# One K tile to a ring tile, 64 bytes behind its head: the split weights of MLA's non-rotary queries and keys

## The chip, the core and the metric

The kernel runs on one core of a Trainium2 chip (8 cores). The core has TensorE (PE; its weight loads are shown as PEld), VectorE (DVE), ScalarE (ACT), GpSimd (POOL) and SyncE (SP), whose queue issues most transfers here. The metric is the device time of one execution in microseconds: 1142.42 us, the median of three runs (1142.38 to 1142.46).

## The reference, cut to what matters

One encoder layer on 256 tokens of width 2048: parallel MLA and differential attention, then cross-attention into 256 memory tokens, a SwiGLU and a final norm, all in float32. The change touches the two up-projections of MLA without rotation:

```
q  = (rms_norm(c_q)  @ w_uq ).reshape(b, s, 8, 128 + 64)    # c_q: 512 wide
q_nope, q_rope = q[..., :128], apply_rope(q[..., 128:], cos_r, sin_r)
kv = (rms_norm(c_kv) @ w_ukv).reshape(b, s, 8, 128 + 128)   # c_kv: 256 wide
k_nope, v_mla = kv[..., :128], kv[..., 128:]
s  = q_nope . k_nope + q_rope . k_rope ;  p = softmax(s * scale) ;  out = p @ v_mla
```

## The kernel before, in words

**Numbers in two halves.** Every float32 operand of a matmul is split into h (a cast to the reduced format fp32r, on ScalarE, line 107) and l (the rest, a subtraction on VectorE, line 108). A product is then three matmuls, in lines 99 to 101: h by h, and the two mixed ones. So TensorE runs three matmuls for each tile of a product, and every weight passes through ScalarE and VectorE before it.

**Weights.** `weights()` (line 124) loads a piece from HBM into a staging buffer `wraw` of 2048 columns, three of which exist, through SP's queue in program order. It then splits it into ring tiles `wh` and `wl` of 1024 columns, four of each. `step` says how many K tiles (128 rows of the contraction) share a ring tile: with 512 columns to a K tile, two. A ring tile is free again when the last matmul that reads it is over; a staging buffer, when the last split that reads it is.

**MLA's up-projections** (lines 605 to 626). First `w_uq_r` (rotary queries, four K tiles, ring tiles wh_791 and wh_795 in the program's numbers) through `project()`, into the PSUM tiles acc_787 and acc_788; the rope of the queries (lines 494 to 498, on VectorE) turns these into qr. Then for each half hg of the heads: `w_uq_n` (four K tiles of 512 columns), `w_ukv_k` (two) and `w_ukv_v` (two). The first two go through `stationary()`: there the weights are the operand that is loaded into TensorE and the transposed activations (cqT, 256 columns) stream past. For each of four heads and each K tile it runs three matmuls of 256 columns: 48 matmuls for qT and 24 for kT per half, 144 in all for both halves. Two heads share one PSUM tile, which is split into qT or kT when all of its matmuls are over. `w_ukv_v` goes through `project()`, where weights stream (512 columns, 12 matmuls).

**Scores.** For each head `scores()` (psc), `softmax()` (maximum on VectorE, exponentials of line 641 on ScalarE, the scaling of e in line 663 on VectorE), `prob_T()` (the transposes ppt, line 652) and `heads_out()` (po). The differential attention's projections (acc from x0T, "dk" the first of those behind) are independent of them.

**What sets the order.** A scheduler goes over the recorded program and orders each engine's instructions by its own estimate of when their operands will be there. Every engine then takes its instructions strictly in that order. Transfers keep the program's order on SP's queue.

Of the kernel before, what the change touches and what calls it, by code (L numbers as in the profile page):

```python
# [12 lines left out]
F32R = mybir.dt.float32r  # L13
# [6 lines left out]
P = 128  # L20
# [60 lines left out]
def encoder_block(ctx: ExitStack, tc: tile.TileContext, a, out):  # L81
# [3 lines left out]
    wp = ctx.enter_context(tc.tile_pool(name="wp", bufs=3))  # L85
# [11 lines left out]
    def mm(o, l, r, start, stop):  # L97

        nc.tensor.matmul(o, l.h, r.h, start=start, stop=False)  # L99
        nc.tensor.matmul(o, l.h, r.l, start=False, stop=False)  # L100
        nc.tensor.matmul(o, l.l, r.h, start=False, stop=stop)  # L101
# [3 lines left out]
    def split_into(dst, src, scale=None, by_vector=False):  # L105
        if scale is None:
            last_cast[0] = nc.scalar.copy(out=dst.h, in_=src).ins  # L107
            last_split[0] = nc.vector.tensor_tensor(out=dst.l, in0=src, in1=dst.h.bitcast(F32), op=ALU.subtract).ins  # L108
        else:
            if by_vector:  # L110
                nc.vector.tensor_scalar(out=dst.h, in0=src, scalar1=scale, scalar2=None, op0=ALU.mult)
            else:
                nc.scalar.activation(dst.h, src, AF.Copy, scale=scale)
            nc.vector.scalar_tensor_tensor(
                out=dst.l, in0=src, scalar=scale, in1=dst.h.bitcast(F32), op0=ALU.mult, op1=ALU.subtract
            )

    def act_tile(shape=(P, 4, S), name="act"):
        return Split(
            act.tile(list(shape), F32R, name=name + "_h", tag="act"),  # L120
            act.tile(list(shape), F32R, name=name + "_l", tag="act"),
        )

    def weights(src, fine=False, pool=None, before_k=None, cut=None, raw=None):

        nk, ncols = src.shape[1:]
        begun = raw is not None  # L130
        if not begun:
            raw = wp.tile([P, 2048], F32, name="wraw", tag="wraw", bufs=3)
        raw = raw[:, :nk * ncols].rearrange("p (k c) -> p k c", k=nk)
        step = 1 if fine else nk
        for k in range(0, nk, step):
            if before_k is not None:
                before_k(k)
            if begun and k == 0:
                continue
            tc.keep_in_program_order(nc.sync.dma_start(out=raw[:, k:k + step, :], in_=src[:, k:k + step, :]))  # L140
        ks = []
        step = max(1, 1024 // ncols // 2 * 2)
        for k in range(0, nk, step):
            n = min(step, nk - k)
            if pool:
                w = pool((P, n, ncols), "w")
            else:
                w = [wp.tile([P, 1024], F32R, name=x, tag=x, bufs=4)[:, :n * ncols].rearrange("p (k c) -> p k c", k=n)
                     for x in ("wh", "wl")]
                w = Split(*w)  # L150
            if fine:
                for j in range(n):
                    for c in ([slice(0, ncols)] if cut is None else [slice(0, cut), slice(cut, ncols)]):
                        split_into(w[:, j, c], raw[:, k + j, c])
            else:
                split_into(w, raw[:, k:k + n, :])
            ks += [w[:, j, :] for j in range(n)]
        return ks

    def project(actT, pieces, before=None, fine=0):  # L160

        accs = [acc_tile() for _ in range(NT)]
        ncols = pieces[0].shape[2]
        nk = sum(src.shape[1] for src in pieces)
        kt = 0
        for i, src in enumerate(pieces):
            if before is not None:
                before(i)
            for w in weights(src, i < fine):
                x = actT(kt)  # L170
                for tt in range(NT):
                    mm(accs[tt][:, :ncols], x[tt] if isinstance(x, tuple) else x[:, tt * P:(tt + 1) * P], w,
                       start=kt == 0, stop=kt == nk - 1)
                kt += 1
        return accs
# [4 lines left out]
    def nat(name):  # L180
        pool, bufs = nat_pool
        return pool.tile([P, 512], F32, name=name, tag="nat", bufs=bufs)
# [8 lines left out]
    def ps_tile(name):  # L191
        pool, tag = banks[1]
        return pool.tile([P, 512], F32, name=name, tag=tag)
# [239 lines left out]
    for i in range(8):  # L433
        one_by_one = i < 3
        if not one_by_one:
            x0T.load(i // 2, i % 2 * 2, 2)
        if i == 3:
            tc.keep_in_program_order(nc.sync.dma_start(out=posi, in_=a["pos"]))
            tc.keep_in_program_order(nc.sync.dma_start(out=invf, in_=a["invf"].partition_broadcast(P)))
        if i >= 6:  # L440
            tc.keep_in_program_order(
                nc.sync.dma_start(out=x_res[i - 6], in_=a["x"][(i - 6) * P:(i - 5) * P, :]))
        for k, w in enumerate(weights(a["w_in_lat"][i], one_by_one,
                                      before_k=lambda k: one_by_one and x0T.load_one(2 * i + k),
                                      cut=QL if i == 0 else None, raw=lat_raw if i == 0 else None)):
            xk = x0T(2 * i + k)
            for tt in range(NT):
                x = xk[:, tt * P:(tt + 1) * P]
                mm(acc_q[tt], x, w[:, :QL], i + k == 0, i == 7 and k == 1)
                mm(acc_kv[tt][:, :LAT], x, w[:, QL:], i + k == 0, i == 7 and k == 1)  # L450
# [49 lines left out]
    def transposed(dst, src, tt, n, gain=None, raw=None):  # L500

        pt = ps_tile("pt")
        for j in range(n):
            nc.tensor.transpose(out=pt[:, j * P:(j + 1) * P], in_=src[:, j * P:(j + 1) * P], identity=ident)  # L504
        pv = pt[:, :n * P].rearrange("p (j t) -> p j t", t=P)
        if gain is not None:
            g = nat("gT").rearrange("p (j t) -> p j t", t=P) if raw is None else raw[:, :, tt * P:(tt + 1) * P]
            nc.vector.tensor_tensor(out=g[:, :n, :], in0=pv, in1=gain.unsqueeze(2).to_broadcast([P, n, P]),
                                    op=ALU.mult)
            pv = g[:, :n, :]  # L510
        split_into(dst[:, :n, tt * P:(tt + 1) * P], pv)
# [14 lines left out]
    cqT = act_tile(name="cqT")  # L526
    lat = act_tile(name="lat")
    ckvT, krT = lat[:, 0:2, :], lat[:, 2:4, :]
# [58 lines left out]
    def values(accs, r=None, n=512):  # L587

        t = act_tile((P, NT, 512), name="val")
        for tt in range(NT):  # L590
            split_into(t[:, tt, :n], accs[tt][:, :n], None if r is None else r[:, tt:tt + 1])
        return t


    def stationary(wk, xT, nk, name):

        t = act_tile(name=name)
        for hp in range(2):
            ps = ps_tile(name)
            for j in range(2):  # L600
                h = hp * 2 + j
                for kt in range(nk):
                    mm(ps[:, j * S:(j + 1) * S], wk[kt][:, h * P:(h + 1) * P], xT[:, kt, :],
                       kt == 0, kt == nk - 1)
            split_into(t[:, 2 * hp:2 * hp + 2, :], ps.rearrange("p (j t) -> p j t", j=2))
        return t
# [7 lines left out]
        qrs.append(qr)  # L614
    qT, kT, vv = [], [], []
    for hg in range(2):
        qT.append(stationary(weights(a["w_uq_n"][hg]), cqT, 4, "qT"))
        if hg == 0:
            for tt in range(NT):
                transposed(qrT, qrs[tt], tt, 4)  # L620
        kT.append(stationary(weights(a["w_ukv_k"][hg]), ckvT, 2, "kT"))
        vv.append(values(project(lambda kt: ckvT[:, kt, :], [a["w_ukv_v"][hg]])))
    mla_split = last_split[0]

# [191 lines left out]
    for tt in range(NT):  # L816
        n = nat("xk")
# [6 lines left out]
    for tt in range(NT):  # L824
        n = nat("xq")
# [113 lines left out]
    for gi, (chunks, order) in enumerate(groups):  # L939
# [5 lines left out]
        src = [a["w_dn"][h, pair0:pair0 + len(hp)] for h in range(2)]  # L945
# [145 lines left out]
```

## Time and profile before

| | |
|---|---|
| median of three runs | 1142.42 us |
| the profiled execution, its own time | 1142.48 us |
| its span | 1140.4 us |
| granted TensorE clock | 0.999 |
| TensorE busy | 1131.3 us, 5393 matmuls |
| VectorE busy | 981.0 us, 1341 instructions |
| ScalarE busy | 649.7 us, 930 instructions |
| qT: matmuls from | 71.46 us on, and again at 83.72 us |
| kT: matmuls from | 80.76 us on |

A row of the order of time has the start in us from the span's start, the length, the engine, the line, and out<-in with shapes; a bracket at the end is the engine's idle time just before and what ended it. In the grouped rows stand the count, the busy time, the mean length in ns, and the idle time before with its releasers. Lengths of matmuls include a part that overlaps the next one; the distance from start to start is what one costs.

### The profile page before, as it was taken

Reading aid. Unit: us, or ns where it says so; the run is one execution under the profiler, and the core shown is the slowest. Engines: PE = TensorE matmul, PEld = TensorE weight load, DVE = VectorE, ACT = ScalarE, POOL = GpSimd, SP = SyncE. Lnnn points to the kernel's source line nnn. Section 1 sums busy time; section 2 is a strip of 40 time slices with the busy share of each in tenths; the row PEclk is TensorE's granted clock in tenths of the full one; section 3 lists DMA queues with packets and bytes.
Section 4 is the critical chain, followed back from the end, with each engine's and each line's share of the span. In section 5 each row is a group of like instructions: output and inputs, shape, how many; then the busy total and the mean of one; then the engine's idle time right before and its main releaser. Section 6 shows DMA issues by size and latency. Waiting matters only on the chain.

```text
span 1140.4 us, 14399 instructions
## 1 busy us (share of the span) xinstructions
PE 1131.3 (99%) x5393; PEld 946.6 (83%) x5393; DVE 981.0 (86%) x1341; ACT 649.7 (57%) x930; POOL 56.4 (5%) x75
## 2 busy tenths in 40 slices
PE   9999999999999999999999999999999999999997
PEld 7888888888888888888888888888888888888886
DVE  6788766878997776989899998998999898998975
ACT  6755455556567555665555464564554664664643
POOL 4920000000001000000000000000000000000000
PEclk9999999999999999999999999999999999999999
DMA  9655334546657445455655555555555655565543
GB/s 351 243 196 183 134 117 145 182 140 227 216 202 272 153 157 182 161 211 187 216 189 216 182 196 217 185 195 211 184 203 203 209 197 195 194 242 204 192 174 129
DMA packets 35493, 222.13 MB, mean 195 GB/s; under 512 B 4320, under 2 KB 5600, under 8 KB 11104
## 3 DMA queue, kind: packets, MB, share of 16 engines
q1 hardware_dynamic: 33696, 216.60, 53.6%
q0 software_dynamic: 864, 3.15, 0.8%
q10 hardware_dynamic: 864, 1.47, 0.4%
q8 instruction: 42, 0.69, 0.2%
q14 instruction: 27, 0.22, 0.1%
HBM read 219.11 MB, written 2.10 MB: 194 GB/s over the span
## 4 chain that ended last, share of the span: by engine, by line
PE 98%; DMA 0%; issue 0%; DVE 0%; ACT 0%; SPq 0%; POOLq 0%; POOL 0%; ACTq 0%
PE acc L99 26%; PE acc L100 26%; PE acc L101 26%; PE q L99 4%; PE q L101 4%; PE q L100 4%; PE pt L504 2%; PE ppt L652 1%; PE psc L101 1%; PE psc L100 1%; PE psc L99 1%; DMA wraw<-in_w_in_lat 0%; PE acckv L99 0%; PE acckv L101 0%; PE pt L924 0%
## 5 line engine op out<-in xcount | busy, mean ns | idle before, releaser
L107 ACT CAST wh<-wraw 128x1024 fp32r<-128x1024 f32 (+2 forms) x401 | 389.4, 990 | 332.9 <-PE acc L101 290.0
L108 DVE TENSOR_TENSOR wl<-wraw,wh 128x1024 fp32r<-128x1024 f32 (+2 forms) x401 | 454.8, 1149 | 90.3 <-ACT wh L107 88.6
L107 ACT CAST wh<-tsum 128x1024 fp32r<-128x1024 f32 (+1 forms) x96 | 96.5, 1006 | 52.7 <-PE acc L101 23.0
L100 PE MATMUL acc<-wl,x2n_h 128*128 128x512 f32 x320 | 124.5, 390 | 0.0
L101 PE MATMUL acc<-wh,x2n_l 128*128 128x512 f32 x320 | 123.9, 389 | 0.0
L108 DVE TENSOR_TENSOR wl<-tsum,wh 128x1024 fp32r<-128x1024 f32 (+1 forms) x96 | 111.5, 1163 | 14.0 <-ACT wh L107 13.8
L99 PE MATMUL acc<-wh,x2n_h 128*128 128x512 f32 x320 | 109.7, 390 | 0.0
L100 PE MATMUL acc<-wl,x0T_h 128*128 128x512 f32 x224 | 88.6, 396 | 0.0
L101 PE MATMUL acc<-wh,x0T_l 128*128 128x512 f32 x224 | 88.2, 394 | 0.0
L99 PE MATMUL acc<-wh,x0T_h 128*128 128x512 f32 x224 | 86.7, 395 | 0.4 <-ACT wh L107 0.3
L100 PE MATMUL acc<-wl,hT_h 128*128 128x512 f32 x188 | 73.3, 392 | 0.0
L100 PE MATMUL q<-wl,forms_h 128*128 128x512 f32 x187 | 72.8, 389 | 0.0
L101 PE MATMUL q<-wh,forms_l 128*128 128x512 f32 x187 | 72.6, 389 | 0.0
L101 PE MATMUL acc<-wh,hT_l 128*128 128x512 f32 x188 | 72.4, 389 | 0.0
L101 PEld LDWEIGHTS acc<-wh,x2n_l 128*128 128x128 f32 x320 | 60.1, 188 | 12.4
L100 PEld LDWEIGHTS acc<-wl,x2n_h 128*128 128x128 f32 x320 | 60.1, 188 | 12.3
L99 PEld LDWEIGHTS acc<-wh,x2n_h 128*128 128x128 f32 x320 | 59.9, 188 | 12.2
L99 PE MATMUL q<-wh,forms_h 128*128 128x512 f32 x187 | 65.6, 389 | 0.0
L100 PE MATMUL acc<-wl,forms_h 128*128 128x512 f32 x167 | 64.8, 389 | 0.0
L101 PE MATMUL acc<-wh,forms_l 128*128 128x512 f32 x167 | 64.8, 389 | 0.0
L99 PE MATMUL acc<-wh,hT_h 128*128 128x512 f32 x188 | 64.5, 391 | 0.0
L99 PE MATMUL acc<-wh,forms_h 128*128 128x512 f32 x167 | 62.9, 389 | 0.0
(406 smaller groups left out, 2240.9 us busy)
## 6 DMA issues: line engine op xcount, KB each, us to landing
wraw<-in_w_gate SPq DMA_DIRECT2D x44, 1024.0 KB, 4.9
wraw<-in_w_up SPq DMA_DIRECT2D x44, 1024.0 KB, 4.8
wraw<-in_w_dn SPq DMA_DIRECT2D x41, 1024.0 KB, 4.9
wraw<-in_w_in SPq DMA_DIRECT2D x24, 1024.0 KB, 4.9
wraw<-in_w_out SPq DMA_DIRECT2D x16, 1024.0 KB, 4.9
wraw<-in_w_in_lat SPq DMA_DIRECT2D x5, 832.0 KB, 7.3
wraw<-in_w_xk SPq DMA_DIRECT2D x4, 1024.0 KB, 5.1
wraw<-in_w_xq SPq DMA_DIRECT2D x4, 1024.0 KB, 5.1
```

Source lines behind the costliest of these rows:

```text
L99: nc.tensor.matmul(o, l.h, r.h, start=start, stop=False)
L100: nc.tensor.matmul(o, l.h, r.l, start=False, stop=False)
L101: nc.tensor.matmul(o, l.l, r.h, start=False, stop=stop)
L107: last_cast[0] = nc.scalar.copy(out=dst.h, in_=src).ins
L108: last_split[0] = nc.vector.tensor_tensor(out=dst.l, in0=src, in1=dst.h.bitcast(F32), op=ALU.subtract).ins
L504: nc.tensor.transpose(out=pt[:, j * P:(j + 1) * P], in_=src[:, j * P:(j + 1) * P], identity=ident)
L652: nc.tensor.transpose(out=pt[:, kt * S + tt * P:kt * S + (tt + 1) * P], in_=p[:, tt, kt * P:(kt + 1) * P], identity=ident)
```

## The change

`weights()` gets a parameter `shift`. Where it is set, one K tile goes into each ring tile instead of two, and it begins `shift` float32 numbers behind the ring tile's head: 16 of them, 64 bytes. Both calls for `stationary()` set it, for w_uq_n and w_ukv_k in both halves. No arithmetic changes, and the staging buffers and transfers stay as they are. (An empty line that the edit adds moves every later line number by one.)

```diff
-    def weights(src, fine=False, pool=None, before_k=None, cut=None, raw=None):
+    def weights(src, fine=False, pool=None, before_k=None, cut=None, raw=None, shift=0):
...
-        step = max(1, 1024 // ncols // 2 * 2)
+        step = 1 if shift else max(1, 1024 // ncols // 2 * 2)
...
-                w = [wp.tile([P, 1024], F32R, name=x, tag=x, bufs=4)[:, :n * ncols].rearrange("p (k c) -> p k c", k=n)
-                     for x in ("wh", "wl")]
+                w = [wp.tile([P, 1024], F32R, name=x, tag=x, bufs=4)[:, shift:shift + n * ncols].rearrange(
+                    "p (k c) -> p k c", k=n) for x in ("wh", "wl")]
...
-        qT.append(stationary(weights(a["w_uq_n"][hg]), cqT, 4, "qT"))
+        qT.append(stationary(weights(a["w_uq_n"][hg], shift=16), cqT, 4, "qT"))
...
-        kT.append(stationary(weights(a["w_ukv_k"][hg]), ckvT, 2, "kT"))
+        kT.append(stationary(weights(a["w_ukv_k"][hg], shift=16), ckvT, 2, "kT"))
```

The scheduler places the instructions anew. SP's and GpSimd's orders are the same as before; those of TensorE, VectorE and ScalarE differ from this place on.

VectorE, before, ahead of the first qT matmul (wraw_837 is the staged first half of w_uq_n; kr_725 is the second token tile's rotary key, pt_734 and pt_720 transposes of keys): both subtractions of the half stand here.

```order
L108 TENSOR_TENSOR wl_840<-wraw_837,wh_839 128x1024
L498 TENSOR_TENSOR kr_725<-kr_725,ropetmp_727 128x64
L108 TENSOR_TENSOR wl_844<-wraw_837,wh_843 128x1024
L508 TENSOR_TENSOR gT_737<-pt_734,gains_101 128x256
L108 TENSOR_TENSOR lat_l_508<-pt_720,lat_h_507 128x2x128
```

So each of the two covers two K tiles, and both lie ahead of the rope of the queries.

VectorE now, in the same region but later: the half has four subtractions, and the fourth one (wl_852) stands behind the rope of the queries, whose last two steps are shown.

```order
L495 TENSOR_TENSOR ropetmp_831<-acc_788,sinr_531 128x8x32
L497 TENSOR_TENSOR qr_830<-acc_788,cosr_530 128x8x32
L108 TENSOR_TENSOR wl_852<-wraw_837,wh_851 128x512
L499 TENSOR_TENSOR qr_823<-qr_823,ropetmp_824 128x512
L499 TENSOR_TENSOR qr_830<-qr_830,ropetmp_831 128x512
L108 TENSOR_TENSOR qT_l_856<-qT_857,qT_h_855 128x512
```

The fourth subtraction moved from ahead of the keys' transposes to behind eight rope steps.

TensorE now, the 15th to the 24th matmul of qT (qT_857 and qT_884 are its two PSUM tiles; wh_847, wh_851 the third and fourth K tile): the matmul that reads wl_852 first is the 23rd.

```order
L99 MATMUL qT_884<-cqT_h_505,wh_847 128x256
L100 MATMUL qT_884<-cqT_l_506,wh_847 128x256
L101 MATMUL qT_857<-cqT_h_505,wl_848 128x256
L101 MATMUL qT_884<-cqT_h_505,wl_848 128x256
L99 MATMUL qT_857<-cqT_h_505,wh_851 128x256
L100 MATMUL qT_857<-cqT_l_506,wh_851 128x256
L99 MATMUL qT_884<-cqT_h_505,wh_851 128x256
L100 MATMUL qT_884<-cqT_l_506,wh_851 128x256
L101 MATMUL qT_857<-cqT_h_505,wl_852 128x256
L99 MATMUL qT_857<-cqT_h_505,wh_839 128x256
```

Before, the heads went one after the other there, all three matmuls of a K tile together.

TensorE before, at the first transposes of probabilities (ppt), which 57 matmuls of the dk projection (acc_1481, acc_1482) precede, the last five of them shown:

```order
L101 MATMUL acc_1482<-wh_1553,x0T_l_297 128x512
L99 MATMUL acc_1481<-wh_1553,x0T_h_296 128x512
L100 MATMUL acc_1481<-wl_1554,x0T_h_296 128x512
L101 MATMUL acc_1481<-wh_1553,x0T_l_297 128x512
L652 MATMUL ppt_1150<-ident_104,e_1142 128x128
L99 MATMUL acc_1482<-wh_1553,x0T_h_296 128x512
```

All four score tiles of the first half stood ahead of these 57.

TensorE now, at the first ppt: the second head's scores (psc_1150) stand directly ahead of it, and the dk projection (acc_1505) begins behind it.

```order
L100 MATMUL psc_1150<-lat_l_508,qrT_h_785 128x256
L101 MATMUL psc_1150<-lat_h_507,qrT_l_786 128x256
L653 MATMUL ppt_1174<-ident_104,e_1166 128x128 x4
L99 MATMUL acc_1505<-wh_1509,x0T_h_118 128x512
L100 MATMUL acc_1505<-wl_1510,x0T_h_118 128x512
```

The first head's transposes moved from behind the dk matmuls to ahead of them.

ScalarE now, the way to those transposes (kT_1079 and kT_1094 are the second half's keys; wh_1509 to wh_1543 weights of dk; e_1166 the exponentials of the first head's scores):

```order
L107 CAST wh_1509<-wraw_1507 128x1024
L107 CAST kT_h_1077<-kT_1079 128x512
L107 CAST wh_1513<-wraw_1507 128x1024
L107 CAST kT_h_1077<-kT_1094 128x512
L642 ACTIVATE e_1166,ssum_1167<-psc_1137,nm_1163 128x256 x2
L107 CAST wh_1543<-wraw_1541 128x1024
L107 CAST val_h_1129<-acc_1109 128x512
```

VectorE's scaling of e_1166 (line 664) stands behind its subtraction for wh_1543. Before, the exponentials stood behind four casts of dk weights.

## The prediction

> **What bounds the kernel now.** I read the page's busy line and its chain of waits first, then the table of stretches, then the order of time around the tiles that the change touches.
>
> ```profile
> span 1140.4 us, 14399 instructions
> PE 1131.3 (99%) x5393; PEld 946.6 (83%) x5393; DVE 981.0 (86%) x1341; ACT 649.7 (57%) x930; POOL 56.4 (5%) x75
> ...
> PE 98%; DMA 0%; issue 0%; DVE 0%; ACT 0%; SPq 0%; POOLq 0%; POOL 0%; ACTq 0%
> ```
>
> TensorE carries 98% of the chain that ended last, so the time is the number of matmuls times their pace, plus the moments in which TensorE waits. The change alters no matmul's shape or count. It can cost or win in two ways only: a wait of TensorE that appears or goes, or a different pace of the matmuls whose weights now stand elsewhere. The stretch it touches:
>
> ```profile
> 71.46:95.00 23.54, 23.54 (x177) 22.54 (x176) 21.30 (x34) 15.97 (x23) 1.56 (x2) 1.00 0.66 226
> ```
>
> In this row (stretch, its length, busy time and count of PE, PEld, DVE, ACT, POOL, then clock, DMA share, GB/s) TensorE has no gap at all: there is no wait here to be won. VectorE is busy 21.30 of 23.54 us, so there is little room for its new work. The pace, from the order of time:
>
> ```profile
> 71.46 0.28 PE L99 MATMUL qT<-cqT_h,wh 128*128 128x256 f32 x1
> ...
> 77.22 0.63 PE L99 MATMUL acc<-wh,lat_h 128*128 128x512 f32 x2
> ...
> 79.97 1.04 PE L504 MATMUL pt<-ident,qr 128*128 128x128 f32 x8
> 80.76 0.36 PE L99 MATMUL kT<-lat_h,wh 128*128 128x256 f32 x1
> ```
>
> The 48 matmuls of qT take 77.22 - 71.46 = 5.76 us, 0.120 each; the 12 of 512 columns 2.75 us, 0.229 each; the eight transposes 0.79 us.
>
> **The change, part by part.** First, the splits. Six pairs of a cast on ScalarE and a subtraction on VectorE become twelve of half the size.
>
> ```profile
> L107 ACT CAST wh<-wraw 128x1024 fp32r<-128x1024 f32 x335 | 346.0, 1052 | 273.4 <-PE acc L101 240.9 <-issue 10.8 <-PE q L101 6.4
> L107 ACT CAST wh<-wraw 128x512 fp32r<-128x512 f32 x50 | 31.0, 621 | 55.5 <-PE acc L101 49.2 <-DMA wraw<-in_w_in_lat 3.0 <-PE q L101 2.5
> L108 DVE TENSOR_TENSOR wl<-wraw,wh 128x1024 fp32r<-128x1024 f32 x335 | 404.1, 1221 | 78.8 <-ACT wh L107 77.5
> L108 DVE TENSOR_TENSOR wl<-wraw,wh 128x512 fp32r<-128x512 f32 x50 | 34.3, 686 | 7.0 <-ACT wh L107 6.6
> ```
>
> ScalarE gets 6 x (2 x 0.621 - 1.052) = 1.1 us more, VectorE 6 x (2 x 0.686 - 1.221) = 0.9 us more. Neither is on the chain by itself: TensorE's own matmuls hide them. What counts is when a split is ready.
>
> Second, the ring. Four of four pairs of ring tiles now hold one half of w_uq_n, where two did. So the fourth K tile can be cast only when the last matmul with w_uq_r (wh_795) is over, just as qT begins. Before, both splits stood long before that.
>
> ```profile
> 70.43 0.27 PE L504 MATMUL pt<-ident,kr 128*128 128x128 f32 x1
> ...
> 69.41 1.05 ACT L107 CAST wh<-wraw 128x1024 fp32r<-128x1024 f32 x1
> 70.74 0.37 ACT L107 CAST lat_h<-pt 128x256 fp32r<-128x256 f32 x1 [0.28 <-PE pt L504]
> 71.70 1.05 ACT L107 CAST wh<-wraw 128x1024 fp32r<-128x1024 f32 x1 [0.59 <-PE acc L101]
> ...
> 70.49 1.23 DVE L108 TENSOR_TENSOR wl<-wraw,wh 128x1024 fp32r<-128x1024 f32 x1 [0.74 <-ACT wh L107]
> 71.64 0.42 DVE L494 TENSOR_TENSOR ropetmp<-acc,sinr 128x256 f32<-128x256 f32 x1
> ...
> 74.62 1.22 DVE L108 TENSOR_TENSOR wl<-wraw,wh 128x1024 fp32r<-128x1024 f32 x1
> 75.75 1.29 DVE L498 TENSOR_TENSOR qr<-qr,ropetmp 128x512 f32<-128x512 f32 x2
> ...
> 327.54 1.22 DVE L108 TENSOR_TENSOR wl<-wraw,wh 128x1024 fp32r<-128x1024 f32 x1
> ...
> 328.82 0.50 PE L100 MATMUL acc<-wl,mT_h 128*128 128x512 f32 x1 [0.19 <-DVE wl L108]
> ```
>
> The casts at 69.41 and 71.70 fill ring tiles of other weights before; now they are K tiles 2 and 3 of the first half. On VectorE the rope of the queries stands between their two subtractions. The third subtraction starts at 69.41 + 0.62 + 0.03 = 70.06 and ends at 70.75. The second kr transpose comes three matmuls of 0.229 earlier, so its cast starts at 70.74 - 0.69 = 70.05, ends at 70.42, and its subtraction runs behind the third one, until about 71.1. From 71.64 to 74.62 VectorE does nine steps of this size, 0.331 each; the eight rope steps thus end at 71.1 + 2.65 = 73.75. Then the fourth subtraction: 0.69, until 74.44, and TensorE starts 0.06 later (328.82 against the end of a subtraction at 327.54 + 1.22 = 328.76, where it waited). TensorE wants it as its 23rd matmul of qT, at 71.46 + 22 x 0.120 = 74.10. **Wait one: 74.50 - 74.10 = 0.4 us.** Everything behind it on TensorE is delayed, since it takes its matmuls in order. Bounds: nothing, if VectorE runs ahead; 0.9 us, if the rope starts at 71.64 as before.
>
> The next places by the same steps: qT ends at 77.62, the transposes at 78.41, kT's first half at 79.85, the values at 82.60, kT at 84.04, the second qT at 89.80. At each place the split is ready, by 0.15 to 0.3 us at four of them: no further term, but a reason for the upper end.
>
> Third, the scores. Before, all four score tiles came late and 57 matmuls of the dk projection covered the softmax. Now the first score tile stands inside kT, and its transposes follow directly behind the second tile, before any dk matmul. ScalarE and VectorE have to be through by then.
>
> ```profile
> 76.25 0.28 PE L100 MATMUL qT<-cqT_l,wh 128*128 128x256 f32 x1
> ...
> 76.62 2.00 ACT L107 CAST wh<-wraw 128x1024 fp32r<-128x1024 f32 x2 [1.50 <-PE qT L100]
> 78.52 0.58 ACT L107 CAST qT_h<-qT 128x512 fp32r<-128x512 f32 x1
> ...
> 83.61 0.57 ACT L107 CAST kT_h<-kT 128x512 fp32r<-128x512 f32 x1
> 84.08 1.08 ACT L107 CAST val_h<-acc 128x512 fp32r<-128x512 f32 x2
> ...
> 104.61 0.46 ACT L641 ACTIVATE e<-psc,nm 128x256 f32<-128x256 f32 x1
> ...
> 105.51 0.47 ACT L641 ACTIVATE e<-psc,nm 128x256 f32<-128x256 f32 x1
> ...
> 106.07 0.62 DVE L663 TENSOR_SCALAR e<-e,rs 128x256 f32<-128x256 f32 x2
> ```
>
> In a row ScalarE needs 0.95 for a cast of 1024 (two until 78.52), 0.47 for one from PSUM (84.08 - 83.61), 0.90 for a tile's two exponentials (105.51 - 104.61). Count from T, the start of the matmul that ends the first kT tile (T is about 93.2). It ends 0.28 later, and a cast follows 0.09 after an end (76.62 against 76.25 + 0.28). Then in ScalarE's new order: kT 0.47, weights 0.95, kT 0.47, exponentials 0.90, weights 1.05; on VectorE 0.03 to start, 1.13 for the subtraction (75.75 - 74.62), 0.35 for the first half of e (0.62 for both), 0.06 to TensorE. Sum 5.78 us. TensorE reaches the transposes after 8 x 0.120 + 2.75 + 12 x 0.120 = 5.15 us. It waits 0.63, and some 0.17 more at the second transpose, whose half of e comes 0.27 later while a transpose takes 0.10. **Wait two: 0.8 us.** Bounds: 0, if ScalarE is ahead of this order; 1.2, if the transfer for its last cast is late.
>
> Fourth, the head of 64 bytes. No row of the profile has weights at such a place: in the built program every ring tile stands 64 bytes past a multiple of 128, and the shifted halves stand on one. The nearest rows are weight loads of two transposes, of x_res (96 bytes past) and e (64 past):
>
> ```profile
> L504 PEld LDWEIGHTS pt<-ident,xres 128*128 128x128 f32 x64 | 7.8, 140 | 1.8
> L652 PEld LDWEIGHTS ppt<-ident,e 128*128 128x128 f32 x64 | 7.9, 140 | 1.4
> ```
>
> Equal, so I take nothing. Bounds: 256 columns more cost 0.229 - 0.120 = 0.109, so 0.011 of a matmul of 0.120 does not scale with its columns; all of it gone from the 144 matmuls of qT and kT is 1.6 us won. On the other side the widest spread of one form is 396 against 390 ns, 144 x 0.006 = 0.9 us lost.
>
> ```profile
> L100 PE MATMUL acc<-wl,x2n_h 128*128 128x512 f32 x320 | 124.5, 390 | 0.0
> L100 PE MATMUL acc<-wl,x0T_h 128*128 128x512 f32 x224 | 88.6, 396 | 0.0
> ```
>
> [...]
>
> Sum: 0.4 + 0.8 + 0 = 1.2 us. The profiled execution took 1142.48 us, 2.1 outside the span; with 1.2 it is 1143.7, and 0.06 less against the median of 1142.42: **1143.6 us**.
>
> **Rivals.** *No wait at all*: the two waits are differences of 0.3 to 0.6 us between chains of 3 to 6 us; if the engines run that much ahead, the time stays 1142.4. For it speaks that TensorE had no gap in this stretch before; against it, VectorE's 90%.
>
> *The head quickens the loads*: 1143.6 - 1.6 = 1142.0. For it speaks the fixed 0.011 us that nothing explains; against it the two equal rows of loads. [...]
>
> *Slower: the staging buffers come free late.* The transfer of the second half of w_uq_n was issued at 67.89, when the first half's last subtraction was over; now that is 74.4. The first dk transfer was issued at 80.09; by the steps above the second half's last subtraction ends at 86.4.
>
> ```profile
> 67.89 0.33 SPq L140 DMA_DIRECT2D wraw<-in_w_uq_n  x1
> ...
> 80.09 31.71 SPq L140 DMA_DIRECT2D wraw<-in_w_in  x7
> ...
> wraw<-in_w_in SPq DMA_DIRECT2D x24, 1024.0 KB, 4.9
> wraw<-in_w_in_lat SPq DMA_DIRECT2D x5, 832.0 KB, 7.3
> ```
>
> At 4.9 us it lands at 91.3, just ahead of ScalarE's turn for it at 91.45. At 7.3, as under the load of the start, it lands at 93.7; the chain of wait two begins 1.1 us late, the next transfer adds 0.5, and the time is 1143.6 + 1.6 = 1145.2. It decides from about 6 us on. Against it: 226 GB/s here, and a median of 4.9.
>
> **Numbers.** My forecast 0.53; no wait 0.17; the quicker head 0.12; late buffers 0.18. A measurement of this kernel tells 0.2%, 2.3 us, from no change: faster means under 1140.1, slower over 1144.7. Even the quicker head without a wait (1140.8) is no change; faster is 0.03. Slower is most of the late buffers and a tail of the forecast: 0.17. The rest, 0.80, is the same. The range goes from 1141.6, the quicker head with a part of the waits, to 1145.4, late buffers.
>
> **What would show it.** Right: TensorE waits for wl (line 108) once early in qT, and for e (line 664) at the first ppt, 0.3 to 1 us each; 144 matmuls at 0.120. Wrong: no idle time of PE between 71 and 100 us (no wait), qT's 48 matmuls in under 5.4 us (the head), a cast that waits for the transfer of w_in (late buffers), or a difference that arises behind 330 us, where I assumed that nothing changes.

## The result: 0.33% slower, and the profile after

| | kernel before | changed kernel |
|---|---|---|
| median of the runs, us | 1142.28 (1141.86 to 1142.46, 6 runs) | 1145.69 (1145.09 to 1147.42, 6 runs) |
| profiled execution, us | 1142.48 | 1145.48 |
| its span, us | 1140.4 | 1143.7 |

The ratio is 1.0033, with a 95% interval from 1.0022 to 1.0043: slower, by more than the 0.2% that can be told from no change. The forecast was 1143.6 with no measurable change, in a range up to 1145.4; the median lies 0.3 us outside.

The busy line and the chain of waits of the changed kernel's page:

```profile
span 1143.7 us, 14416 instructions
PE 1132.7 (99%) x5393; PEld 947.1 (83%) x5393; DVE 981.4 (86%) x1347; ACT 648.7 (57%) x936; POOL 56.5 (5%) x75
...
PE 96%; DVE 1%; ACT 1%; issue 1%; DMA 0%; POOL 0%; POOLq 0%; SPq 0%; ACTq 0%
```

TensorE's share of the chain falls from 98 to 96%; VectorE and ScalarE enter it. The table of what TensorE waited for (70 to 103 us: total, times, longest), empty for the kernel before in this stretch, names them:

```profile
PE qT L101 <- DVE wl L108: 1.6, 2, 1.4
PE ppt L653 <- DVE e L664: 0.7, 1, 0.7
```

These idle times count from the modelled end of a matmul. What a wait costs is better read from start to start. TensorE's order of time at the three places:

```profile
73.82 0.28 PE L100 MATMUL qT<-cqT_l,wh 128*128 128x256 f32 x1
74.28 0.38 PE L101 MATMUL qT<-cqT_h,wl 128*128 128x256 f32 x1 [0.18 <-DVE wl L108]
74.50 0.28 PE L99 MATMUL qT<-cqT_h,wh 128*128 128x256 f32 x1
...
85.08 0.28 PE L101 MATMUL qT<-cqT_h,wl 128*128 128x256 f32 x1
...
86.38 0.28 PE L100 MATMUL qT<-cqT_l,wh 128*128 128x256 f32 x1
88.03 0.38 PE L101 MATMUL qT<-cqT_h,wl 128*128 128x256 f32 x1 [1.37 <-DVE wl L108]
88.25 0.28 PE L99 MATMUL qT<-cqT_h,wh 128*128 128x256 f32 x1
...
99.52 0.28 PE L101 MATMUL psc<-lat_h,qrT_l 128*128 128x256 f32 x1
100.45 0.72 PE L653 MATMUL ppt<-ident,e 128*128 128x128 f32 x4 [0.65 <-DVE e L664]
101.22 0.50 PE L99 MATMUL acc<-wh,x0T_h 128*128 128x512 f32 x1
101.56 0.40 PE L100 MATMUL acc<-wl,x0T_h 128*128 128x512 f32 x1
```

- **Pace.** From 85.08 to 86.38 eleven matmuls of qT start 0.118 us apart, where the kernel before had 0.120. Over all 144 matmuls of qT and kT the records give 2.1 ns each, 0.30 us won.
- **Wait one** (first qT): (74.50 - 73.82) - 2 x 0.118 = 0.44 us.
- **A wait in the second qT**, which the prediction did not have: (88.25 - 86.38) - 2 x 0.118 = 1.63 us.
- **Wait two** (first ppt): (100.45 - 99.52) - 0.12 = 0.81 for e. Behind it two more things follow. In the records one transpose behind another costs 0.109 and a matmul behind a transpose starts 0.028 later (7 x 0.109 + 0.028 makes the 0.79 of the eight transposes in the prediction), so four should take 0.36 to the next matmul's start. They take 0.77: 0.12 more between the first three, the second of which waits for its half of e, and 0.29 more behind the last. The 0.29 is a wait of its own, which the table above leaves out because it stands at a weight load: the first dk matmul has to wait until VectorE has read its accumulator for val_l. That matmul then takes 0.34 instead of 0.23, 0.11 more. Together 0.81 + 0.12 + 0.29 + 0.11 = 1.33 us.

```profile
101.22 0.19 PEld L99 LDWEIGHTS acc<-wh,x0T_h 128*128 128x128 f32 x1 [0.29 <-DVE val_l L108]
```

At all three places the first matmul behind the wait costs 0.10 to 0.11 us more than its pace (0.22 instead of 0.118 twice, 0.34 instead of 0.23); this is counted above.

So 0.44 + 1.63 + 1.33 - 0.30 = 3.10 of the 3.3 us by which the span grew; the remaining 0.2 is a sum of small gaps of both signs elsewhere, the largest at 284 us (0.57 more than the pace, where TensorE waits for a cast) and at 328 us (0.35 less).

What held the second qT stands in VectorE's order of time, and behind it GpSimd's and SyncE's queue (a view each, in this order):

```profile
73.54 0.69 DVE L108 TENSOR_TENSOR wl<-wraw,wh 128x512 fp32r<-128x512 f32 x1
...
77.34 2.60 DVE L108 TENSOR_TENSOR wl<-wraw,wh 128x512 fp32r<-128x512 f32 x3
...
84.05 1.29 DVE L108 TENSOR_TENSOR wl<-wraw,wh 128x512 fp32r<-128x512 f32 x2
86.95 0.42 DVE L692 TENSOR_REDUCE ldot<-lamv 128x2 f32<-128x256 f32 x1 [1.61 <-POOL lamv L690]
87.29 0.68 DVE L108 TENSOR_TENSOR wl<-wraw,wh 128x512 fp32r<-128x512 f32 x1
```

```profile
86.19 0.73 POOL L690 TENSOR_TENSOR lamv<-lamv 128x256 f32<-128x256 f32 x1 [20.60 <-DMA lamv<-in_lam]
```

```profile
79.97 0.33 SPq L141 DMA_DIRECT2D wraw<-in_w_ukv_v  x1
80.35 0.42 SPq L689 DMA_DIRECT2D lamv<-in_lam  x1
...
88.00 18.50 SPq L141 DMA_DIRECT2D wraw<-in_w_in  x5
```

`lamv` are the four lambda vectors of differential attention. GpSimd multiplies them in pairs (line 690), VectorE sums the products into `ldot` (line 692). The work belongs to a later stage; the scheduler puts the sum into VectorE's queue here, ahead of the subtraction for the fourth K tile (line 108 at 87.29). All casts for these subtractions were over at 84.83 (the last three on ScalarE from 83.17, 1.66 us), but VectorE, in its order, took the sum first: the subtraction that TensorE wanted at 86.5 stood behind a sum that waited 1.61 us for GpSimd, which waited for the transfer. That transfer was issued at 80.35, right behind the staging transfer of w_ukv_v. And that one went out at 79.97, as soon as a staging buffer was free: the three subtractions from 77.34 end at 79.94. In the kernel before the same transfer went out at 76.24 and the same product ran at 80.45. SyncE's and GpSimd's rows of before, then its table of who waited for lamv and the time to its landing, and that time in the changed kernel:

```profile
76.24 0.42 SPq L688 DMA_DIRECT2D lamv<-in_lam  x1
```

```profile
80.45 0.74 POOL L689 TENSOR_TENSOR lamv<-lamv 128x256 f32<-128x256 f32 x1 [14.21 <-PE acc L101]
```

```profile
  DVE ldot L691: 0.6, 1
...
DMA to landing us min/median/max: 3.7/3.7/3.7
```

```profile
DMA to landing us min/median/max: 5.3/5.3/5.3
```

VectorE waited for GpSimd there too, 0.6 us, with nothing behind it that TensorE was short of. Four microseconds later at the issue, 5.3 instead of 3.7 us to the landing, and a sum that now stands ahead of an urgent subtraction: that is the wait of 1.63 us.

### The profile page after: what moved, and what is told of

Its sections match the earlier page's. It is cut to its first block, busy times and chain, and to the rows that moved or that the text cites. A ratio compares the mean times of both kernels' runs of the same rounds, so it can differ in the third digit from the quotient of the medians.

```text
span 1143.7 us, 14416 instructions
## 1 busy us (share of the span) xinstructions
PE 1132.7 (99%) x5393; PEld 947.1 (83%) x5393; DVE 981.4 (86%) x1347; ACT 648.7 (57%) x936; POOL 56.5 (5%) x75
## 4 chain that ended last, share of the span: by engine, by line
PE 96%; DVE 1%; ACT 1%; issue 1%; DMA 0%; POOL 0%; POOLq 0%; SPq 0%; ACTq 0%
PE acc L99 26%; PE acc L100 26%; PE acc L101 26%; PE q L99 4%; PE q L101 4%; PE q L100 4%; PE pt L505 2%; ACT wh L107 1%; PE ppt L653 1%; PE psc L100 1%; PE psc L101 1%; PE psc L99 1%; DVE wl L108 0%; DMA lamv<-in_lam 0%; PE acckv L99 0%
## 5 line engine op out<-in xcount | busy, mean ns | idle before, releaser
L100 PE MATMUL acc<-wl,x2n_h 128*128 128x512 f32 x320 | 124.5, 390 | 0.0
```

## The experiments

All are compared with the kernel before on the same chip in the same session (median 1141.9 to 1142.05). An execution outlasts its span by 1.7 to 2.2 us where both are known.

**1. The lambda transfer on another queue.** One word of the changed kernel:

```
-    tc.keep_in_program_order(nc.sync.dma_start(out=lamv, in_=a["lam"].partition_broadcast(P)))
+    tc.keep_in_program_order(nc.gpsimd.dma_start(out=lamv, in_=a["lam"].partition_broadcast(P)))
```

> The changed kernel with one difference: the transfer of the four lambda vectors is issued by GpSimd and no longer by SyncE, where it stands behind two staging transfers that wait for subtractions. TensorE's order is the same. Theory 1 (the 1.6 us wait of TensorE in the second qT is VectorE's: it stands at the lambda sum ldot, for GpSimd's product, for this transfer, ahead of the subtraction that TensorE wants): the wait at 86.4 us goes whole, no VectorE wait for lamv is left, and the time falls by 1.6 us to 1144.1, ratio to before 1.0016; the waits at 73.8 (0.44) and 99.5 (0.9 to 1.2) stay. Theory 2 (the ring of four frees its tile too late, and the casts with it): the wait stays at 1 us or more although ldot is done early, 1145.2 to 1145.7.

1143.64 us, ratio 1.0014 (1.0005 to 1.0022): 2.0 us less than the changed kernel, where 1.6 were expected. The table of what TensorE waited for, then the transfer and the product on GpSimd:

```profile
PE ppt L652 <- DVE e L663: 0.7, 1, 0.7
PE qT L101 <- DVE wl L108: 0.2, 1, 0.2
```

```profile
68.55 0.79 POOL L688 DMA_DIRECT2D lamv<-in_lam  x1 [2.99 <-PE pt L504]
72.20 0.74 POOL L689 TENSOR_TENSOR lamv<-lamv 128x256 f32<-128x256 f32 x1 [2.86 <-DMA lamv<-in_lam]
```

The product is there 14 us earlier; the sum runs at 75.31, waits for nothing and holds nothing up, and the wait of the second qT is gone whole; the two predicted waits stay. Theory 1 holds: 1.6 of the 3.3 us are the lambda vectors'. (The spans of the two profiled executions differ by 1.5 us, 1143.7 against 1142.2, so the 2.0 between the medians is no sign of a further gain.) The scheduler also moved the sum forward in VectorE's order, so this run does not tell the late transfer from the place of the sum; experiment 5 does.

**2. One K tile to a ring tile, without the head.**

```
-                w = [wp.tile([P, 1024], F32R, name=x, tag=x, bufs=4)[:, shift:shift + n * ncols].rearrange(
+                w = [wp.tile([P, 1024], F32R, name=x, tag=x, bufs=4)[:, :n * ncols].rearrange(
```

> The changed kernel without the head: one K tile to a ring tile, at the ring tile's own start. The order on every engine is that of the changed kernel. Theory 1 (the ring alone makes the three waits, the head makes the 256-column matmuls 0.118 instead of 0.120 us): the same three waits, the pace of the 144 matmuls of qT and kT back at 0.120, time 1145.7 + 144 x 0.0022 = 1146.0. Theory 2 (the head costs): 1144 or less. Theory 3 (the head does nothing, the pace moved by chance): 0.118 here too.

1145.6 us (1.0026 to 1.0051): the loss is all there. The waits (wait one is there too, 0.41 us from start to start, too short an idle time for the table), and the pace between 85.02 and 85.98 (eight steps, 0.120 each):

```profile
PE qT L101 <- DVE wl L108: 1.2, 1, 1.2
PE ppt L652 <- DVE e L663: 1.2, 1, 1.2
```

```profile
85.02 0.28 PE L101 MATMUL qT<-cqT_h,wl 128*128 128x256 f32 x1
...
85.98 0.28 PE L100 MATMUL qT<-cqT_l,wh 128*128 128x256 f32 x1
87.48 0.39 PE L101 MATMUL qT<-cqT_h,wl 128*128 128x256 f32 x1 [1.23 <-DVE wl L108]
```

The order makes the waits, which are here without the head; the pace goes with the head (0.118 with it, 0.120 without). The 0.3 us of the head do not show between 1145.6 and 1145.69; the waits themselves differ by more (the second qT 1.49 instead of 1.63, the step to the first ppt 0.5 longer, behind a cast that waited 1.64 us for w_in instead of 1.04).

**3. The first transfer of w_in in two halves**, on top of experiment 1 (the DMA of that one piece goes out as two of 512 KB):

```
-        step = 1 if fine else nk
+        step = 1 if fine else dma or nk        # dma=2 for the first piece of dk, 0 elsewhere
```

> The kernel with the lambda transfer on GpSimd's queue, and in it the first 1024 KB transfer of w_in for the dk projection as two of 512 KB, since the cast that waited 1.13 us for it reads the first half alone. TensorE's order is the same; ScalarE casts the second half one place earlier. Theory 1 (the wait of TensorE for the softmax, 0.90 + 0.45 us, comes from that transfer: its buffer is free late): the cast no longer waits, or under 0.3 us, the wait at the first ppt falls to 0.3 us or less in all, 1143.6 - 1.0 = 1142.6. Theory 2 (the chain of ScalarE's own work is what is too long, as the prediction had it): ScalarE waits elsewhere, the wait at the first ppt stays at 0.8 or more, 1143.2 to 1143.6.

1143.73 us (1.0005 to 1.0023), no gain over experiment 1. ScalarE's order of time in experiment 1, then in this one:

```profile
92.30 1.05 ACT L107 CAST wh<-wraw 128x1024 fp32r<-128x1024 f32 x1 [1.13 <-DMA wraw<-in_w_in]
```

```profile
93.18 0.59 ACT L107 CAST kT_h<-kT 128x512 fp32r<-128x512 f32 x1 [0.97 <-PE kT L101]
```

The transfer was late, as theory 1 had it; taking that away only lets ScalarE wait for TensorE's kT instead. TensorE's step from the last score to the first ppt goes from 98.79 - 97.78 = 1.01 to 98.73 - 97.87 = 0.86 us:

```profile
97.78 0.28 PE L101 MATMUL psc<-lat_h,qrT_l 128*128 128x256 f32 x1
98.79 0.72 PE L652 MATMUL ppt<-ident,e 128*128 128x128 f32 x4 [0.74 <-DVE e L663]
```

```profile
97.87 0.28 PE L101 MATMUL psc<-lat_h,qrT_l 128*128 128x256 f32 x1
98.73 0.72 PE L652 MATMUL ppt<-ident,e 128*128 128x128 f32 x4 [0.59 <-DVE e L663]
```

The late transfer was worth 0.15 us of wait two. Theory 2, the chain of ScalarE's own work behind kT, is the cause of the wait for e. The wait for val_l behind the transposes is here as before, 0.29 us.

**4. One staging buffer for two small transfers**, on top of experiment 1. The second w_ukv_k and w_ukv_v go into one tile of 2048 columns:

```
+        both = [None, None]
+        if hg in (1,):
+            both = wp.tile([P, 2048], F32, name="wraw", tag="wraw", bufs=3)
+            both = [both[:, :1024], both[:, 1024:]]
...
-        kT.append(stationary(weights(a["w_ukv_k"][hg], shift=16), ckvT, 2, "kT"))
+        kT.append(stationary(weights(a["w_ukv_k"][hg], shift=16, raw=both[0]), ckvT, 2, "kT"))
```

> The kernel with the lambda transfer on GpSimd's queue, and in it the second halves of w_ukv_k and w_ukv_v (512 KB each) in one staging buffer instead of two, so that the first transfer of w_in for dk finds a buffer free some 8 us earlier. The scheduler then also puts the first ppt behind matmuls of dk. Theory 1 (all the loss but wait one comes from buffers that are free late): only the wait in the first qT is left, 0.44, less 0.3 for the quicker 256-column matmuls: 1142.0 to 1142.4. Theory 2 (the softmax chain is itself too late): a wait of 0.5 us or more for e stays, 1143 or more.

1143.28 us, 1.0011 (1.0002 to 1.0020). The first transfer of w_in now goes out at 79.84 instead of 85.90. TensorE still stops at the same place, but for something else:

```profile
79.84 12.34 SPq L140 DMA_DIRECT2D wraw<-in_w_in  x3
```

```profile
PE acc L99 <- DVE val_l L108: 0.5, 1, 0.5
PE qT L101 <- DVE wl L108: 0.2, 1, 0.2
```

With the transposes moved behind, the first matmul of dk is next, and it wants an accumulator that VectorE's val_l has yet to read: the wait that stood behind the transposes in the changed kernel. Neither theory is met word for word: the wait for e is gone, and one of 0.5 us stands in its place, from the same crowded VectorE.

**5. One part of the change alone**: `shift=16` on w_uq_n only, and on w_ukv_k only.

> The change to w_uq_n alone; w_ukv_k stays two K tiles to a ring tile. VectorE then has both subtractions of the second half's first two K tiles and those of the other two ahead of the lambda sum ldot. Theory (each wait has its own place): wait one stays as it was, 0.4 us in all; no wait in the second qT, since the lambda sum now stands behind all four subtractions of it; the head gains 96 x 0.0022 = 0.2 us; a wait of 0 to 0.9 us at the first ppt. 1142.1 to 1143.2. Rival (the second qT waits for its ring tile as such): a wait of 1 us or more there, 1143.5 or more.

> The change to w_ukv_k alone; w_uq_n stays two K tiles to a ring tile, so the first qT has its splits as early as before. The lambda sum stands ahead of the subtraction for K tiles 3 and 4 of the second qT. Theory: no wait one; a wait in the second qT only if the lambda transfer lands later than about 83 us; the head gains 48 x 0.0022 = 0.1 us; 1142.0, same as before. Rival (wait one comes from the ring's rotation, whichever half is shifted): 0.4 us in the first qT here too. If the lambda transfer lands as late as with the whole change (86 us), a wait of 1.5 us and 1143.5.

The queries alone: 1143.57 us, 1.0014 (1.0005 to 1.0023). The keys alone: 1141.91 us, 1.0000 (0.9991 to 1.0009). The table of what TensorE waited for has, with the queries alone, the same two lines as in experiment 4 (0.5 us for val_l, 0.2 for wl); with the keys alone it is empty.

Wait one belongs to the split of w_uq_n: with the queries alone it is there as before (0.34 + 0.10 us in the records), with the keys alone it is not. With the queries alone the lambda sum stands behind all the subtractions of the second qT, and the large wait is gone, though the transfer is nearly as late as ever (79.80); with the keys alone the sum waits 0.64 us for GpSimd, TensorE loses 0.29 us in the second qT, and nothing of it shows in the time:

```profile
83.70 0.42 DVE L691 TENSOR_REDUCE ldot<-lamv 128x2 f32<-128x256 f32 x1 [0.64 <-POOL lamv L689]
```

The range for the queries, 1142.1 to 1143.2, was missed by 0.4: a wait for an accumulator at 98 us, and short ones at kT, were not in it.

**6. The head alone, and its control.** To keep two K tiles behind a head, ring tiles need 32 columns more (the same 1056 at the two other places where the kernel makes ring tiles):

```
-        step = 1 if shift else max(1, 1024 // ncols // 2 * 2)
+        step = max(1, 1024 // ncols // 2 * 2)
...
-                w = [wp.tile([P, 1024], F32R, name=x, tag=x, bufs=4)[:, shift:shift + n * ncols].rearrange(
+                w = [wp.tile([P, 1056], F32R, name=x, tag=x, bufs=4)[:, shift:shift + n * ncols].rearrange(
```

> The kernel before with the head alone: the halves of w_uq_n and w_ukv_k stand 64 bytes behind the start of their ring tile, still two or four K tiles to a tile; every ring tile is 128 bytes longer so that all other operands keep their place within 128 bytes. The order on every engine is that of the kernel before. Theory 1 (the place of the weights sets the pace): 144 matmuls at 0.118, no wait in TensorE, 1142.3 - 0.3 = 1142.0. Theory 2 (no effect): 0.120 and 1142.3. Theory 3 (the head causes the loss): 1144 or more.

1155.2 us, 1.0115 (1.0101 to 1.0129), with no wait of TensorE anywhere near: 13 us that no theory had. So the longer tiles were run without a head (the same, without `shift=16`):

> The control to the run with the head alone, which took 1155.2: the kernel before with every ring tile 128 bytes longer, and no head. Theory 1 (the loss of 13 us is of the longer ring tiles: the 512-column matmuls take 0.230 instead of 0.227 us because tiles no longer start at the same place within 4096 bytes): 1155 here too, qT and kT at 0.113 to 0.120. Theory 2 (the loss is of the head): 1142.1.

1155.25 us, 1.0115 (1.0099 to 1.0130): the 13 us are the longer tiles'. TensorE's busy time, and one group of 512 columns, of the run with the head:

```profile
PE 1144.4 (99%) x5393; PEld 946.3 (82%) x5393; DVE 983.2 (85%) x1341; ACT 649.0 (56%) x930; POOL 56.9 (5%) x75
...
L100 PE MATMUL acc<-wl,x2n_h 128*128 128x512 f32 x320 | 125.6, 394 | 0.0
```

The control has the same 1144.4 and 125.6, 394. The group took 124.5 us and 390 ns before. The matmuls of 512 columns are slower on average, also the 30 whose weights stand in pT tiles instead of ring tiles (226.7 ns from start to start before, 229.3 in the control). With the head qT starts every 0.114 us (0.1136 in the mean; 0.1186 in the control), quicker than the 0.118 of the changed kernel. That need not come from the longer tiles: in experiment 1, whose edit moves no tile of the changed kernel, the first qT goes at 0.118 up to wait one and at 0.113 behind it to its end (15 steps between these two rows), and the second at 0.118 again:

```profile
75.16 0.28 PE L99 MATMUL qT<-cqT_h,wh 128*128 128x256 f32 x1
...
76.86 0.28 PE L101 MATMUL qT<-cqT_h,wl 128*128 128x256 f32 x1
```

So the same places allow two paces. No run here shows what picks one of them.

**7. Where the rings stand.** Two edits tell place from distance. All operands moved together by 64 bytes:

```
-    gains = const.tile([P, 74], F32, name="gains")
+    gains = const.tile([P, 90], F32, name="gains")[:, :74]
```

> The kernel before with 64 bytes more in the tile of the gains, so that every operand of a matmul in SBUF starts on a multiple of 128 bytes, where all stood 64 past one. The order on every engine is that of the kernel before. Theory 1 (a matmul loses 2 ns where its weights stand 64 bytes past a multiple of 128, of whatever width): 4475 matmuls of 512 columns and 506 of 256 gain 0.0024 us each, 12 us, 1130. Theory 2 (only those of 256 columns, for which the weight load is the longer part): 506 x 0.0024 = 1.2 us, 1141.1. Theory 3 (what counts is that weights and moving operand stand differently): no change, 1142.3, pace 0.120.

And everything behind the rings moved against them, by 16, 32 or 64 columns of 4 bytes:

```
+    wp.tile([P, 16], F32, name="apart", tag="apart", bufs=1)
     qrT = act_tile(name="qrT")
```

> The kernel before with 64 bytes between the rings of the weights and all tiles behind them: weights keep their place 64 bytes past a multiple of 128, the activations stand on a multiple of 128. The order on every engine is that of the kernel before. Theory 1 (a matmul's pace goes by the distance of its moving operand from the weights that are loaded meanwhile, in the low bits of the address): qT and kT at 0.118 as in the changed kernel, and the 4475 matmuls of 512 columns move too, by 2 to 4 ns each, 1131 to 1133 if down, 1151 to 1160 if up. Theory 2 (only the 256-column matmuls go by it): 1142.05 - 144 x 0.0022 = 1141.7. Theory 3 (no effect): 1142.05.

> As the run with 64 bytes between the rings and the tiles behind them (1167.0), but 128 bytes. The order on every engine is that of the kernel before. Theory 1 (the distance counts within 128 bytes): 1142, the 512-column matmuls at 0.227, qT and kT at 0.120. Theory 2 (it counts within 256 or 512 bytes): the 512-column matmuls at 0.230 to 0.233, 1155 or more.

> As the runs with 64 and 128 bytes between the rings and the tiles behind them (1167.0 and 1164.2), but 256 bytes. In the kernel before, the 394 matmuls of 512 columns whose operands stand an odd multiple of 256 bytes apart run at 0.2269 us, no slower than the rest. Theory 1 (only the distance within 256 bytes counts): 1142.0, 512 columns at 0.227, qT and kT at 0.120. Theory 2 (any shift of the rings against the rest costs, whatever its size): 0.230 or more and 1155 or more.

The order in the last three is that of the kernel before up to 340 us; behind that a few matmuls of the summed blocks change places, which the third of them shows to cost nothing. TensorE's busy line of each, in this order: all together, then 64, 128 and 256 apart.

```profile
PE 1131.8 (99%) x5393; PEld 947.2 (83%) x5393; DVE 980.8 (86%) x1341; ACT 649.8 (57%) x930; POOL 57.1 (5%) x75
```

```profile
PE 1156.3 (99%) x5393; PEld 945.5 (81%) x5393; DVE 984.9 (85%) x1341; ACT 648.7 (56%) x930; POOL 56.9 (5%) x75
```

```profile
PE 1153.7 (99%) x5393; PEld 949.3 (82%) x5393; DVE 985.2 (85%) x1341; ACT 648.8 (56%) x930; POOL 56.3 (5%) x75
```

```profile
PE 1130.9 (99%) x5393; PEld 946.4 (83%) x5393; DVE 980.7 (86%) x1341; ACT 649.6 (57%) x930; POOL 55.9 (5%) x75
```

| run | time, us | ratio (95%) | 512 columns, ns | qT, ns |
|---|---|---|---|---|
| before | 1142 | | 227 | 120 |
| changed kernel | 1145.69 | 1.0033 (1.0022 to 1.0043) | 227 | 118 |
| all moved by 64 bytes | 1142.1 | 1.0000 (0.9991 to 1.0009) | 227 | 120 |
| rings 64 apart | 1167.01 | 1.0219 (1.0205 to 1.0233) | 233 | 118 |
| rings 128 apart | 1164.17 | 1.0193 (1.0177 to 1.0208) | 232 | 119 |
| rings 256 apart | 1141.95 | 1.0001 (0.9992 to 1.0011) | 227 | 120 |
| tiles 128 bytes longer | 1155.25 | 1.0115 (1.0099 to 1.0130) | 230 | 119 |
| the same, with the head | 1155.2 | 1.0115 (1.0101 to 1.0129) | 230 | 114 |

The last two columns are mean distances from start to start in the records, without gaps. All moved together met Theory 3; the rings 64 apart Theory 1, upwards and past its 1160; 128 apart Theory 2; 256 apart Theory 1. Moving all operands together by 64 bytes did not count (1142.1 us); moving the rings against the rest by 64 or 128 bytes did (1167.01 and 1164.17), and 256 bytes counted as none (1141.95). The longer tiles fit in: if they stand one behind the other, at 4224 bytes each, every second one starts an odd multiple of 128 bytes from where it was; half of the matmuls at 232.4 ns and half at 227.3 make 229.9, an estimate from the two runs, and 230.4 were measured. No run beat the kernel before.

## Why the prediction was wrong

- **"Wait one 0.4 us."** Right in place and cause, and in size partly by luck: 0.44, of which 0.34 lies ahead of the 23rd matmul and 0.10 behind it, a slow first step that the prediction had no term for. It waited for the subtraction that ends at 74.23 by the row of VectorE (73.54 + 0.69; predicted 74.44, with everything on TensorE 0.1 earlier too). The keys alone do not have it.
- **"At each place the split is ready … no further term."** This is the step that failed, for 1.63 of the 2.1 us that the forecast lacked. The steps gave every subtraction its own time on VectorE and named neither the lambda sum among them nor what it waits for. The order showed it between two subtractions of the second qT; the trace of before had it waiting for GpSimd already, with nothing urgent behind it. What the changed order did was to put an urgent subtraction behind it, and the later staging transfers delayed the lambda transfer by four microseconds on SyncE's queue. Both facts could be had beforehand: the prediction wrote of transfers that staging buffers hold back, but followed only w_in's, not the small one that stands between them.
- **"Wait two 0.8 us."** The mechanism was right for e (experiment 3), and nearly the size: 0.81 instead of 0.63 to the first transpose, of which 0.15 is the late transfer, by experiment 3, and 0.12 between the transposes instead of 0.17. But the place costs 1.33, past the upper bound of 1.2. The prediction stopped at the transposes: it had no term for the first dk matmul behind them, which waits 0.29 for val_l to be read out of its accumulator, nor for the slow step behind a wait, 0.11.
- **"The head … I take nothing."** Not nothing, but within its bounds: 0.30 us won, 2.1 ns on each of 144 matmuls. The two equal rows of weight loads that spoke against it were not the right witnesses: those transposes read x_res and e, 32 bytes apart within 128, and their loads are equal (140 ns), while matmuls of qT and kT start closer with the head than without it (0.118 against 0.120, experiment 2). The place of the weights against the rest does show in the pace: rings moved by 64 or 128 bytes against the rest made a matmul of 512 columns 5 to 6 ns slower (experiment 7).
- **The rival of the late staging buffers** was half real. The first transfer of w_in was issued at 88.00 (86.4 was the estimate) and ScalarE waited 1.04 us for it in the changed kernel. Its price of 1.6 us was wrong: ScalarE would have waited for kT instead, and experiment 3 gives 0.15. The time that this rival named, 1145.2, was nearly right, for another reason.
- **A difference behind 330 us, "where I assumed that nothing changes".** The assumption held: from 360 us on no stretch of 20 us differs by more than 0.1.
- **The range** left out waits at places that had slack by the count: four places with 0.15 to 0.3 us each were named as "a reason for the upper end", but no term stood for a wait of the engine ahead of them.

By the sum: 1.2 was forecast; 0.04 more at wait one, 0.53 at wait two's place, 1.63 at the lambda sum, 0.3 less by the head and 0.2 elsewhere make 3.3.

## What to carry to other kernels

When an edit changes the order on an engine that is 90% busy, go through every instruction that now stands ahead of an urgent one, ask what each waits for and follow that back through its queue: a small piece of a later stage can cost more than all the work that was added (1.63 us here, against 0.9 us of new work on VectorE). Do not stop at the wait that was found: the next instruction behind it can have a wait of its own, as the dk matmul had. A staging buffer that comes free later delays what stands behind it in the queue that issues, not only its own successor (lamv went out 4.11 us later here, at 80.35 instead of 76.24). Before a ring tile gets a head or other padding, look at what it does to the distance between rings and activations (256 bytes cost nothing here, 64 and 128 cost 25 and 22 us), and run a control with the padding alone.

## What was not expected of the hardware

Moving the weight rings by 64 or 128 bytes against the activations made the 4476 matmuls of 512 columns 5 to 6 ns slower on average (227 to 233 and 232 ns), 25 and 22 us of the kernel, while those of qT and kT, with 256 columns and ring weights as the loaded operand, became 1 to 2 ns faster; 256 bytes changed nothing (experiment 7). The 256-column matmuls of MLA's scores, which read no ring tile, stayed at 119.5 ns. Ring tiles 128 bytes longer cost 3 ns for each 512-column matmul (experiment 6). The granted clock was 0.998 to 0.999 in all of these runs, so it is not the clock.

Nor is it the writes of ScalarE and VectorE into other ring tiles. With the rings 64 bytes apart, nine matmuls of 512 columns between 1126.89 and 1128.75 us start 0.233 apart, while VectorE, ScalarE and GpSimd do nothing at all (the row of that stretch, with columns as in the prediction):

```profile
1126.89:1128.75 1.86, 1.86 (x9) 1.50 (x8) 0.00 (x0) 0.00 (x0) 0.00 (x0) 1.00 0.58 189
```

By the records of that run, 43 matmuls of 512 columns with these three engines idle go at 233.4 ns, 1169 with no transfer under way at 233.1, and all at 233.1. So the loss is there with no other engine at work. What is left is the place of TensorE's own operands, the weights it loads against those that stream, which these edits moved; that is argued from what was ruled out, and no run shows how the place costs time. It stays open, too, why wide and narrow matmuls move in opposite directions, and why the 30 matmuls whose weights stand in pT tiles, outside the rings, also went from 226.7 to 231.5 ns with the rings 64 apart.
